# Block-diagonal compressed keys and values, a compression in two stretches, and a later place for the split of h, in a two-layer hybrid decoder trunk

## The chip, the cores and the metric

The kernel runs on one core of one Trainium2 chip. The metric is the device time of one execution, in microseconds. The engines by their names in the profile: PE is the matrix engine (PEld its weight loads), DVE the vector engine, ACT the scalar engine, POOL the GpSimd engine, and SP the engine that issues most DMAs. Each engine takes its instructions in the order in which the program has them.

## The reference, cut to what matters

256 positions of width 1024 go through two layers; each layer is a SwiGLU half-step, a token mixer and a second SwiGLU half-step. All is float32.

```python
def swiglu(x, w_gate, w_up, w_down):
    return (silu(x @ w_gate) * (x @ w_up)) @ w_down      # D_FF = 2816

for l in range(2):
    x = x + 0.5 * swiglu(rms_norm(x, norm_ffn1[l]), ...)
    x = x + hybrid_mixer(rms_norm(x, norm_mix[l]), ...)
    x = x + 0.5 * swiglu(rms_norm(x, norm_ffn2[l]), ...)
return rms_norm(x, norm_final)
```

The mixer has four groups of four heads of 64: forgetting attention (fox), native sparse attention (NSA), sliding-window (swa) and dilated attention (dil). NSA sums three gated branches; the one that the change touches is the compressed branch. Its keys and values are 15 compressed positions, made by a small MLP over windows of 32 positions, and all four heads share them:

```python
blocks = concat(chunks[:-1], chunks[1:]) + cmp_pe[idx]        # 15 windows of 32 positions x 64
kc, vc = silu(blocks . cmp_w1[idx]) @ cmp_w2[idx]             # 15 x 64, once for k, once for v
p_cmp = masked_softmax(q . kc / 8 - slope * dist, dist >= 0)  # 256 x 15 for each of 4 heads
o_cmp = gate0 * (p_cmp @ vc)
```

## The kernel before, in words

The positions are two halves (h = 0 and 1) of 128 rows. Every weight matrix is cut into sets of 256 rows by up to 512 columns. For each set, SP loads `wraw` (one of four buffers), ACT rounds it to a high part `whi` (fp32r), DVE computes the rest, `wlo` (line 115 is `split`, lines 119 to 121, which does both; line 149 is the matmul of `Set.mm`). The activations are split alike (`xhi`, `xlo`, `hhi`, `hlo`), and a product is the sum of three matmuls for each 128 rows: hi by hi, hi by lo and lo by hi. A set is so six matmuls for one half, twelve for both. Sets are split two ahead of their use (`AHEAD`), and the work of half 1 follows that of half 0 by five sets (`LAG`). A tile `whi` or `wlo` is free for a new set when half 1 has used the old one.

An FFN goes in 11 chunks of 256 hidden columns. A chunk is four sets of gate and up (`gate_up`, accumulating in the bank `ps_g`) and two sets of down for the chunk two before it (`down_`, banks `ps_d`). After the fourth gate-up set, ACT computes SiLU (line 318, `sg`), DVE multiplies (line 319), and the product h must be turned before it is an operand of down. In chunks 0, 1 and 10 PE turns it (`turn`, line 290). In the eight others it goes a far way (`turn_far`): DVE transposes blocks of 32 (`z`, line 298), POOL writes four pieces to DRAM (`far`, line 301) and reads them back (`pT`, line 305), and after a counted number of steps (`BACK`) the split of h is written into the program:

```python
            yield BACK
            back = back.rearrange("p (a k i) -> p k a i", a=4, k=2)
            hT[h, c] = tuple(hbuf.tile([P, 2, P], F32R, name=f"h{t}{h}") for t in ("hi", "lo"))
            split(back, *(t.rearrange("p k (a i) -> p k a i", a=4) for t in hT[h, c]))
```

A tile scheduler then places the instructions of each engine by a modelled due time; `tc.issue_after(x)` makes it place what stands under it behind x on the same engine.

The mixer projects its input by the sets of `win` and runs the attention beside them: generators (`attend`, `compress`, `cmp_branch`, ...) advance by one step with each set. `attend` computes scores (line 399, two heads at a time in 64-row halves of the array), a softmax, scaling by 1/sum (DVE), four transposes (line 445), a copy to `pT` (line 448) and the products with the values (line 457). `compress` loads four pieces of `cmp_w1` into `wraw` buffers, with eight matmul pairs for each (line 497), and makes from them `kc` and `vc` (lines 504 to 520). `idle` (line 95) is the operand of the matmuls that warm PE up at the start.

Of the kernel before, what the change touches and what calls it, by code (L numbers as in the profile page):

```python
# [15 lines left out]
P = 128  # L16
# [6 lines left out]
NB = 15  # L23
# [32 lines left out]
def hybrid_kernel(ctx: ExitStack, tc: tile.TileContext, a: dict, out: bass.AP):  # L56
# [27 lines left out]
    tbl = {g: const.tile([P, 4, 2 * P], F32, name=f"tbl_{g}") for g in ("nsa", "swa", "dil")}  # L84
    tbl["tri"] = const.tile([P, P], F32, name="tbl_tri")
# [9 lines left out]
    idle = const.tile([P, P], mybir.dt.bfloat16, name="idle")  # L95
    nc.vector.memset(idle, 0.0)
# [14 lines left out]
    def keep(engine, f, *args, **kw):  # L111

        last = fixed.get(engine)
        with tc.issue_after(last.ins) if last is not None else nullcontext():
            ins = f(*args, **kw)  # L115
        if engine in fixed:
            fixed[engine] = ins

    def split(pt, hi, lo):
        keep("ACT", nc.scalar.activation, hi, pt, AF.Copy)  # L120
        keep("DVE", nc.vector.tensor_tensor, lo, pt, hi.bitcast(F32), op=ALU.subtract)

    class Set:
# [5 lines left out]
        def load(self, parts=1):  # L129
# [8 lines left out]
            for k in ks:  # L138
                yield
                split(r[:, k], self.hi[:, k], self.lo[:, k])  # L140
# [140 lines left out]
    def add_ffn(norm, gu, down, nxt):  # L281
# [12 lines left out]
        def turn_far(h, c, hh):  # L294
# [14 lines left out]
            split(back, *(t.rearrange("p k (a i) -> p k a i", a=4) for t in hT[h, c]))  # L309
# [34 lines left out]
    def add_mixer(l, norm, nxt):  # L344
# [57 lines left out]
        def softmax(h, views, table, nk, sink=None, guard=False):  # L402

            p = work.tile([P, 4, P * (h + 1)], F32, name=f"p{h}")[:, :, :nk]
# [77 lines left out]
        def compress():  # L482
# [8 lines left out]
            for q in range(4):  # L491
                w1 = raw.tile([P, 2, 512], F32, name="wraw").rearrange("p j (c e) -> p j c e", e=P)
                nc.sync.dma_start(w1, a["w1"][l, q])
                yield 2
                for j in range(2):
                    for c in range(4):
                        nc.tensor.matmul(part[32 * c:32 * c + NB, :P], blk[:, c // 2, 8 * (c % 2) + 2 * q + j, :],
                                         w1[:, j, c, :], start=q == 0 and j == 0, stop=q == 3 and j == 1)
# [18 lines left out]
            kc = small.tile([P, NB], F32, name="kc", bufs=1)  # L517
            nc.vector.tensor_copy(kc, cp[:, :NB])
            M["vc"] = small.tile([NB, 64], F32, name="vc", bufs=1)
            nc.vector.tensor_copy(M["vc"], cp[:NB, 64:128])  # L520
            M["kc"] = kc

        def cmp_branch(h):
            while "kc" not in M:
                yield 1
# [334 lines left out]
```

## Time and profile before

| what | value |
|---|---|
| time, median of 3 runs | 1019.8 us (1019.18 to 1020.0) |
| time of the profiled execution | 1020.97 us |
| its span in the profile | 1019.2 us |
| PE busy | 996.3 us (98%) |
| DVE, ACT, POOL busy | 642.0, 515.8, 195.0 us |
| DMA | 200.36 MB, 197 GB/s on average |
| mean granted clock of PE | 0.995 |

The time of an execution is the span and 1.8 us around it. The profiled execution lies 1.2 us above the median of the three runs. A row of the timeline begins with its start and its duration in us; a matmul of 512 columns is shown for 0.39 us, but matmuls are pipelined, so what counts is the distance from one start to the next. In brackets stands how long the engine had been idle, and what ended that.

### The profile page before, as it was taken

The numbers are of one execution on the slowest core, as the hardware profiler recorded it, in microseconds if no ns is written. First come the engines' busy times: TensorE is split into PE (matmuls) and PEld (weight loads), VectorE is DVE, ScalarE is ACT, GpSimd is POOL, SyncE is SP. The second block draws the span as 40 slices with busy tenths as digits, with TensorE's granted clock in tenths as the row PEclk, the third lists the DMA queues.
The fourth block names the chain that finished last, engine by engine and source line by source line (L and its number), as shares of the span: only waits on it lengthen the run. The fifth ranks groups of instructions, "written<-read, shape, count | busy, mean of one in ns | idle before, by whom it ended". The sixth has DMA issues, their size and how long they took to land.

```text
span 1019.2 us, 14178 instructions
## 1 busy us (share of the span) xinstructions
PE 996.3 (98%) x4899; PEld 801.4 (79%) x4899; DVE 642.0 (63%) x1223; ACT 515.8 (51%) x886; POOL 195.0 (19%) x351
## 2 busy tenths in 40 slices
PE   8999999999999999999999999999999999999997
PEld 5788787867778888788878888878678788888875
DVE  6565656786777456465755565648776775656464
ACT  6444444554665445354644454446466564445452
POOL 0132323010000023332102232310100001323230
PEclk9999999999999999999999999999999999999999
DMA  8677767644354466676656777755634455677671
GB/s 294 235 224 262 235 220 244 207 151 166 119 166 139 154 212 215 219 221 237 204 175 202 222 229 224 235 186 176 189 109 155 128 166 190 205 234 214 220 232 47
DMA packets 68855, 200.36 MB, mean 197 GB/s; under 512 B 12448, under 2 KB 20528, under 8 KB 68784
## 3 DMA queue, kind: packets, MB, share of 16 engines
q1 hardware_dynamic: 56352, 180.83, 55.1%
q0 software_dynamic: 11712, 17.86, 5.4%
q8 instruction: 38, 0.62, 0.3%
q10 hardware_dynamic: 720, 0.79, 0.2%
q14 instruction: 33, 0.27, 0.1%
HBM read 189.98 MB, written 9.45 MB: 196 GB/s over the span
## 4 chain that ended last, share of the span: by engine, by line
PE 40%; DMA 26%; DVE 11%; POOL 9%; issue 7%; ACT 7%; POOLq 0%; SPq 0%; ACTq 0%; DVEq 0%
PE ps_g L149 22%; DMA far<-z 13%; DMA pT<-far 11%; PE ps_d L149 10%; POOL far L301 9%; DVE wlo L115 5%; ACT whi L115 4%; PE ps_t L457 2%; DVE sg L319 2%; DMA wraw<-in_gu 1%; PE ps_t L445 1%; DVE z L298 1%; PE ps_d L399 1%; PE ps_t L379 1%; PE ps_t L262 1%
## 5 line engine op out<-in xcount | busy, mean ns | idle before, releaser
L115 DVE TENSOR_TENSOR wlo<-wraw,whi 128x1024 fp32r<-128x1024 f32 (+3 forms) x329 | 392.4, 1196 | 176.6 <-ACT whi L115 175.6
L115 ACT ACTIVATE whi<-wraw 128x1024 fp32r<-128x1024 f32 (+3 forms) x329 | 341.0, 1038 | 224.9 <-PE ps_g L149 105.4
L149 PE MATMUL ps_g<-whi,xhi 128*128 128x512 f32 (+2 forms) x896 | 352.0, 394 | 5.8 <-ACT whi L115 3.8
L149 PE MATMUL ps_g<-wlo,xhi 128*128 128x512 f32 (+2 forms) x896 | 347.5, 388 | 3.7 <-DVE wlo L115 3.6
L149 PE MATMUL ps_g<-whi,xlo 128*128 128x512 f32 (+2 forms) x896 | 346.4, 387 | 0.0
L149 PEld LDWEIGHTS ps_g<-whi,xhi 128*128 128x128 f32 x896 | 168.6, 188 | 47.5 <-ACT whi L115 6.7
L301 POOL DMA_DIRECT2D far<-z x256 | 139.8, 554 | 327.4 <-DVE z L298 322.8
L149 PEld LDWEIGHTS ps_g<-wlo,xhi 128*128 128x128 f32 x896 | 168.7, 188 | 37.3 <-DVE wlo L115 6.8
L149 PEld LDWEIGHTS ps_g<-whi,xlo 128*128 128x128 f32 x896 | 168.5, 188 | 31.7 <-DVE xlo L115 0.5
L149 PE MATMUL ps_d<-whi,hhi 128*128 128x512 f32 x352 | 138.9, 395 | 0.0
L149 PE MATMUL ps_d<-whi,hlo 128*128 128x512 f32 x352 | 137.8, 391 | 0.0
L149 PE MATMUL ps_d<-wlo,hhi 128*128 128x512 f32 x352 | 137.6, 391 | 0.0
L115 ACT ACTIVATE hhi<-pT 128x256 fp32r<-128x256 f32 x64 | 26.7, 417 | 153.4 <-DMA pT<-far 153.4
L115 DVE TENSOR_TENSOR hlo<-pT,hhi 128x256 fp32r<-128x256 f32 x64 | 27.2, 425 | 107.5 <-ACT hhi L115 107.4
L149 PEld LDWEIGHTS ps_d<-whi,hlo 128*128 128x128 f32 x352 | 66.4, 189 | 13.9
L149 PEld LDWEIGHTS ps_d<-wlo,hhi 128*128 128x128 f32 x352 | 66.6, 189 | 13.6
L149 PEld LDWEIGHTS ps_d<-whi,hhi 128*128 128x128 f32 x352 | 66.5, 189 | 13.4
L159 POOL TENSOR_TENSOR rstd<-ms,mhalf 128x1 f32<-128x1 f32 x14 | 8.6, 614 | 291.4 <-DVE ms L157 291.4
L305 POOL DMA_DIRECT2D pT<-far x64 | 35.6, 557 | 142.4 <-DMA far<-z 111.9
L318 ACT ACTIVATE sg<-ps_g,rstd 128x256 f32<-128x256 f32 x88 | 41.1, 467 | 22.4 <-PE ps_g L149 22.1
L319 DVE SCALAR_TENSOR_TENSOR sg<-ps_g,rstd,sg 128x256 f32<-128x256 f32 x88 | 42.1, 478 | 15.8 <-ACT sg L318 15.8
L416 ACT ACTIVATE p<-p,nm 128x128 f32<-128x128 f32 (+2 forms) x96 | 40.1, 419 | 22.8 <-DVE nm L408 10.5
(158 smaller groups left out, 654.4 us busy)
## 6 DMA issues: line engine op xcount, KB each, us to landing
wraw<-in_gu SPq DMA_DIRECT2D x175, 512.0 KB, 4.1
wraw<-in_down SPq DMA_DIRECT2D x88, 512.0 KB, 4.5
wraw<-in_win SPq DMA_DIRECT2D x24, 512.0 KB, 4.0
far<-z POOLq DMA_DIRECT2D x256, 32.0 KB, 4.0
pT<-far POOLq DMA_DIRECT2D x64, 128.0 KB, 3.7
wraw<-in_wout SPq DMA_DIRECT2D x16, 512.0 KB, 3.5
wraw<-in_win SPq DMA_DIRECT2D x16, 384.0 KB, 3.6
wraw<-in_w SPq DMA_DIRECT2D x8, 512.0 KB, 3.5
```

What stands on the lines that cost most here:

```text
L115: ins = f(*args, **kw)
L149: nc.tensor.matmul(acc, x_[k], w[:, k, :], start=first and i == 0, stop=last and i == 5)
L262: nc.tensor.transpose(pt[:, j, :], xg[:, j * P:(j + 1) * P], ident)
L298: nc.vector.transpose(st, hh)
L301: nc.gpsimd.dma_start(far[:, :, a_, :].rearrange("b j e -> j b e"), st[32 * a_:32 * a_ + 32].rearrange("j (b e) -> j b e", b=4))
L305: nc.gpsimd.dma_start(back, far.rearrange("b j a e -> (b j) (a e)"))
L318: nc.scalar.activation(sg, acc[h][:, :256], AF.Silu, scale=r)
L319: nc.vector.scalar_tensor_tensor(sg, acc[h][:, 256:], r, sg, op0=ALU.mult, op1=ALU.mult)
L379: nc.tensor.transpose(pt[:, j, :], z[:, j * P:(j + 1) * P], ident)
L399: nc.tensor.matmul(dst, qT[r, i // 2, :], keys(i)[r, :nk], start=True, stop=True)
L416: nc.scalar.activation(p[:, i, :], p[:, i, :], AF.Exp, bias=nm[:, i:i + 1], scale=-1.0, accum_out=den[:, i:i + 1])
L457: nc.tensor.matmul(o[64 * e:64 * e + 64, j, :], vals(2 * j + e, n), pts[n][:w, 2 * j + e, :], start=n == 0, stop=n == len(blocks) - 1)
```

## The change

It has four parts.

1. In the far chunks the split of h is tied to the split of the set that was split last when the program comes to that point: `split` and `keep` now return their ACT instruction, each set keeps it as `last`, and `turn_far` issues h's split under `tc.issue_after`.
2. The compressed branch. `kc` becomes a tile of 128 x 2 x 15 in which the keys of the even heads stand in rows 0 to 63 and those of the odd heads in rows 64 to 127, in columns of their own, the rest zero. `vc` becomes a 128 x 256 tile with the values in four blocks, at rows 32 i and at the columns of head i, the rest zero. The probabilities of the four heads stand side by side in a constant tile `pc`, 32 columns for each head. So the scores take one matmul for two heads, the transposes become one of 128 x 128, and the products with the values one matmul for two heads. The scaling by 1/sum is one DVE instruction over four heads instead of four.
3. `compress` loads two pieces of `cmp_w1` and then runs the matmuls of both, and does so twice, where before each of the four pieces had its matmuls one step after its load.
4. The warm-up matmuls read the zeroed tile `ph` instead of a tile of their own.

```diff
--- before.py
+++ after.py
@@ -82,6 +82,8 @@
     ph = const.tile([P, P], F32, name="ph")
     nc.gpsimd.memset(ph, 0.0)
     tbl = {g: const.tile([P, 4, 2 * P], F32, name=f"tbl_{g}") for g in ("nsa", "swa", "dil")}
+    pc = const.tile([P, 4, 32], F32, name="pc")
+    nc.gpsimd.memset(pc, 0.0)
     tbl["tri"] = const.tile([P, P], F32, name="tbl_tri")
     tbl["cmp"] = const.tile([P, 2, 4, NB], F32, name="tbl_cmp")
 
@@ -92,8 +94,7 @@
                 nc.sync.dma_start(tbl[g] if dst is None else dst, a[f"c_{g}"])
 
 
-    idle = const.tile([P, P], mybir.dt.bfloat16, name="idle")
-    nc.vector.memset(idle, 0.0)
+    idle = ph.bitcast(mybir.dt.bfloat16)[:, :P]
     one = const.tile([P, 1], F32, name="one")
     nc.vector.memset(one, 1.0)
     heat = bank("t")
@@ -115,10 +116,12 @@
             ins = f(*args, **kw)
         if engine in fixed:
             fixed[engine] = ins
+        return ins
 
     def split(pt, hi, lo):
-        keep("ACT", nc.scalar.activation, hi, pt, AF.Copy)
+        first = keep("ACT", nc.scalar.activation, hi, pt, AF.Copy)
         keep("DVE", nc.vector.tensor_tensor, lo, pt, hi.bitcast(F32), op=ALU.subtract)
+        return first
 
     class Set:
 
@@ -137,7 +140,7 @@
                 self.dma = nc.sync.dma_start(r[:, k], self.src[:, k])
             for k in ks:
                 yield
-                split(r[:, k], self.hi[:, k], self.lo[:, k])
+                self.last = split(r[:, k], self.hi[:, k], self.lo[:, k])
 
         def mm(self, acc, hi, lo, first, last):
             xs = ((hi, self.hi), (hi, self.lo), (lo, self.hi))
@@ -306,7 +309,8 @@
             yield BACK
             back = back.rearrange("p (a k i) -> p k a i", a=4, k=2)
             hT[h, c] = tuple(hbuf.tile([P, 2, P], F32R, name=f"h{t}{h}") for t in ("hi", "lo"))
-            split(back, *(t.rearrange("p k (a i) -> p k a i", a=4) for t in hT[h, c]))
+            with tc.issue_after(sets[done[0] - 1].last.ins):
+                split(back, *(t.rearrange("p k (a i) -> p k a i", a=4) for t in hT[h, c]))
 
         def gate_up(h, c, s, st):
             if s == 0:
@@ -399,9 +403,10 @@
                 nc.tensor.matmul(dst, qT[r, i // 2, :], keys(i)[r, :nk], start=True, stop=True)
             return views
 
-        def softmax(h, views, table, nk, sink=None, guard=False):
-
-            p = work.tile([P, 4, P * (h + 1)], F32, name=f"p{h}")[:, :, :nk]
+        def softmax(h, views, table, nk, sink=None, guard=False, p=None):
+
+            if p is None:
+                p = work.tile([P, 4, P * (h + 1)], F32, name=f"p{h}")[:, :, :nk]
             nm = small.tile([P, 4], F32, name="nm")
             den = small.tile([P, 4], F32, name="den")
             for i in (0, 2, 1, 3):
@@ -488,14 +493,17 @@
                     nc.vector.tensor_tensor(blk[r, v], src,
                                             M["pe"][r, v, :].unsqueeze(2).to_broadcast([64, 16, NB]), op=ALU.add)
             part = bank("d1")
-            for q in range(4):
-                w1 = raw.tile([P, 2, 512], F32, name="wraw").rearrange("p j (c e) -> p j c e", e=P)
-                nc.sync.dma_start(w1, a["w1"][l, q])
-                yield 2
-                for j in range(2):
-                    for c in range(4):
-                        nc.tensor.matmul(part[32 * c:32 * c + NB, :P], blk[:, c // 2, 8 * (c % 2) + 2 * q + j, :],
-                                         w1[:, j, c, :], start=q == 0 and j == 0, stop=q == 3 and j == 1)
+            for qs in ((0, 1), (2, 3)):
+                w1 = []
+                for q in qs:
+                    w1.append(raw.tile([P, 2, 512], F32, name="wraw").rearrange("p j (c e) -> p j c e", e=P))
+                    nc.sync.dma_start(w1[-1], a["w1"][l, q])
+                    yield 2
+                for q in qs:
+                    for j in range(2):
+                        for c in range(4):
+                            nc.tensor.matmul(part[32 * c:32 * c + NB, :P], blk[:, c // 2, 8 * (c % 2) + 2 * q + j, :],
+                                             w1[q % 2][:, j, c, :], start=q == 0 and j == 0, stop=q == 3 and j == 1)
             for c in range(4):
                 r = slice(32 * c, 32 * c + NB)
                 nc.vector.tensor_copy(ph[r], part[r, :P])
@@ -514,17 +522,43 @@
             nc.tensor.matmul(cp[:, :NB], M["w2"][:, 0:2, :].rearrange("p t d -> p (t d)"), hid[:, 0, :],
                              start=True, stop=True)
             nc.tensor.matmul(cp[:NB, 64:128], hid[:, 1, :], M["w2"][:, 2, :], start=True, stop=True)
-            kc = small.tile([P, NB], F32, name="kc", bufs=1)
-            nc.vector.tensor_copy(kc, cp[:, :NB])
-            M["vc"] = small.tile([NB, 64], F32, name="vc", bufs=1)
-            nc.vector.tensor_copy(M["vc"], cp[:NB, 64:128])
+
+            kc = small.tile([P, 2, NB], F32, name="kc", bufs=1)
+            nc.gpsimd.memset(kc, 0.0)
+            M["vc"] = work.tile([P, 2, 16, NB], F32, name="blk", bufs=1).rearrange("p a b c -> p (a b c)")[:, :256]
+            nc.gpsimd.memset(M["vc"], 0.0)
+            for e in range(2):
+                r = slice(64 * e, 64 * e + 64)
+                nc.vector.tensor_copy(kc[r, e, :], cp[r, :NB])
+            for i in range(4):
+                c = 128 * (i // 2) + 64 * (i % 2)
+                nc.vector.tensor_copy(M["vc"][32 * i:32 * i + NB, c:c + 64], cp[:NB, 64:128])
             M["kc"] = kc
 
         def cmp_branch(h):
+
             while "kc" not in M:
                 yield 1
-            yield from attend(h, lambda: M["nq", h], lambda i: M["kc"], lambda i: tbl["cmp"][:, h, i, :],
-                              lambda i, n: M["vc"], put_part(h, False, True), NB, f"d{h}", gate=0, guard=True)
+            s = bank(f"d{h}")[:, :4 * NB].rearrange("p (j e k) -> p j e k", j=2, e=2)
+            for j in range(2):
+                nc.tensor.matmul(s[:, j].rearrange("p e k -> p (e k)"), M["nq", h][:, j, :],
+                                 M["kc"].rearrange("p e k -> p (e k)"), start=True, stop=True)
+            p, rd = softmax(h, [s[:, :, e, :] for e in range(2)], lambda i: tbl["cmp"][:, h, i, :], NB,
+                            guard=True, p=pc[:, :, :NB])
+            w = small.tile([P, 4], F32, name="gw")
+            nc.vector.tensor_tensor(w, rd, M["gate", h][:, 0::3], op=ALU.mult)
+            nc.vector.tensor_tensor(p, p, w.unsqueeze(2).to_broadcast([P, 4, NB]), op=ALU.mult)
+            yield 3 + 2 * h
+            yield 0
+            pt = bank("t")
+            nc.tensor.transpose(pt[:, :P], pc.rearrange("p i k -> p (i k)"), ident)
+            sb = work.tile([P, 4, P], F32, name="pT")[:, 0, :]
+            nc.scalar.activation(sb, pt[:, :P], AF.Copy)
+            yield 2
+            o = bank("t")[:, :256].rearrange("p (j t) -> p j t", j=2)
+            for j in range(2):
+                nc.tensor.matmul(o[:, j, :], M["vc"][:, P * j:P * j + P], sb, start=True, stop=True)
+            put_part(h, False, True)(o)
 
         def log_sigmoid(h, z, r):
```

ACT early in the first FFN, before. `hhi1` and `hhi0` are the high parts of an h of half 1 and of one of half 0, both from the far way (`pT`); `sg` are two SiLUs:

```order
L115 ACTIVATE whi_608<-wraw_607 128x1024
L115 ACTIVATE hhi1_694<-pT_577 128x256
L115 ACTIVATE whi_627<-wraw_626 128x1024
L115 ACTIVATE hhi0_704<-pT_586 128x256
L115 ACTIVATE whi_645<-wraw_644 128x1024
L318 ACTIVATE sg_662<-ps_g_600,rstd_227 128x256
L115 ACTIVATE whi_673<-wraw_672 128x1024
L318 ACTIVATE sg_684<-ps_g_613,rstd_199 128x256
L115 ACTIVATE whi_709<-wraw_708 128x1024
```

The same nine rows after the change:

```order
L116 ACTIVATE whi_608<-wraw_607 128x1024
L116 ACTIVATE whi_627<-wraw_626 128x1024
L116 ACTIVATE whi_645<-wraw_644 128x1024
L322 ACTIVATE sg_662<-ps_g_600,rstd_227 128x256
L116 ACTIVATE whi_673<-wraw_672 128x1024
L116 ACTIVATE hhi1_694<-pT_577 128x256
L322 ACTIVATE sg_684<-ps_g_613,rstd_199 128x256
L116 ACTIVATE hhi0_704<-pT_586 128x256
L116 ACTIVATE whi_709<-wraw_708 128x1024
```

`hhi1` passed three `whi` and a `sg`, `hhi0` two `whi` and both `sg`.

DVE at the same place, before (`hlo` is the low part of h, `z` the blockwise transpose of the product that begins the far way):

```order
L115 TENSOR_TENSOR hlo1_695<-pT_577,hhi1_694 128x256
L115 TENSOR_TENSOR wlo_628<-wraw_626,whi_627 128x1024
L115 TENSOR_TENSOR hlo0_705<-pT_586,hhi0_704 128x256
L115 TENSOR_TENSOR wlo_646<-wraw_644,whi_645 128x1024
L319 SCALAR_TENSOR_TENSOR sg_662<-ps_g_600,rstd_227,sg_662 128x256
L298 STREAM_TRANSPOSE z_665<-sg_662 128x256
L115 TENSOR_TENSOR wlo_674<-wraw_672,whi_673 128x1024
L319 SCALAR_TENSOR_TENSOR sg_684<-ps_g_613,rstd_199,sg_684 128x256
L298 STREAM_TRANSPOSE z_687<-sg_684 128x256
L115 TENSOR_TENSOR wlo_710<-wraw_708,whi_709 128x1024
```

And after:

```order
L116 TENSOR_TENSOR wlo_646<-wraw_644,whi_645 128x1024
L323 SCALAR_TENSOR_TENSOR sg_662<-ps_g_600,rstd_227,sg_662 128x256
L301 STREAM_TRANSPOSE z_665<-sg_662 128x256
L116 TENSOR_TENSOR wlo_674<-wraw_672,whi_673 128x1024
L323 SCALAR_TENSOR_TENSOR sg_684<-ps_g_613,rstd_199,sg_684 128x256
L116 TENSOR_TENSOR hlo1_695<-pT_577,hhi1_694 128x256
L301 STREAM_TRANSPOSE z_687<-sg_684 128x256
L116 TENSOR_TENSOR hlo0_705<-pT_586,hhi0_704 128x256
L116 TENSOR_TENSOR wlo_710<-wraw_708,whi_709 128x1024
```

`hlo1` now stands between the second product and its `z`, and `hlo0` behind that `z`.

PE where half 0 has its compressed scores in the first layer, before (`ps_d0<-kc`), and where their transposes and those of another head group stand:

```order
L149 MATMUL ps_g_2334<-whi_2027,xhi11_1796 128x512
L149 MATMUL ps_g_2334<-wlo_2028,xhi11_1796 128x512
L399 MATMUL ps_d0_2374<-kc_2370,qT_1928 128x15
L399 MATMUL ps_d0_2375<-kc_2370,qT_1928 128x15
L399 MATMUL ps_d0_2374<-kc_2370,qT_1928 128x15
L399 MATMUL ps_d0_2375<-kc_2370,qT_1928 128x15
L149 MATMUL ps_g_2334<-whi_2027,xlo11_1797 128x512
L379 MATMUL ps_t_2422<-ident_86,z_2413 128x128 x2
L399 MATMUL ps_d1_2444<-kT_win_1808,qT_2110 128x256
L379 MATMUL ps_t_2422<-ident_86,z_2413 128x128 x2
L445 MATMUL ps_t_2430<-ident_86,p1_2315 128x128 x4
```

After:

```order
L152 MATMUL ps_g_2334<-whi_2027,xhi11_1796 128x512
L152 MATMUL ps_g_2334<-wlo_2028,xhi11_1796 128x512
L152 MATMUL ps_g_2334<-whi_2027,xlo11_1797 128x512
L544 MATMUL ps_d0_2380<-kc_2370,qT_1928 128x30 x2
L383 MATMUL ps_t_2421<-ident_86,z_2412 128x128 x2
L403 MATMUL ps_d1_2443<-kT_win_1808,qT_2110 128x256
L403 MATMUL ps_d1_2444<-kT_win_1808,qT_2110 128x256
L450 MATMUL ps_t_2429<-ident_86,p1_2315 128x128 x4
```

The four score matmuls have become two, one matmul of the projection later, and stand next to the transposes of line 379 (383 after).

PE at the second piece of `cmp_w1`, before (`ps_d1<-wraw,blk`; line 445 are transposes of the window branch):

```order
L445 MATMUL ps_t_2194<-ident_86,p0_2133 128x128
L149 MATMUL ps_g_2032<-whi_2084,xhi01_1727 128x512
L564 MATMUL ps_t_2095<-upper_89,lf_2078 4x128
L445 MATMUL ps_t_2194<-ident_86,p0_2133 128x128 x3
L149 MATMUL ps_g_2032<-wlo_2085,xhi01_1727 128x512
L149 MATMUL ps_g_2032<-whi_2084,xlo01_1728 128x512
L149 MATMUL ps_g_2032<-whi_2084,xhi01_1727 128x512
L149 MATMUL ps_g_2032<-wlo_2085,xhi01_1727 128x512
L149 MATMUL ps_g_2032<-whi_2084,xlo01_1728 128x512
L497 MATMUL ps_d1_2117<-wraw_2179,blk_2112 15x128 x8
L149 MATMUL ps_g_2152<-whi_1901,xhi11_1796 128x512
L149 MATMUL ps_g_2152<-wlo_1902,xhi11_1796 128x512
```

After:

```order
L152 MATMUL ps_g_2032<-whi_2084,xhi01_1727 128x512
L152 MATMUL ps_g_2032<-wlo_2085,xhi01_1727 128x512
L450 MATMUL ps_t_2186<-ident_86,p0_2133 128x128
L152 MATMUL ps_g_2032<-whi_2084,xlo01_1728 128x512
L598 MATMUL ps_t_2095<-upper_89,lf_2078 4x128
L450 MATMUL ps_t_2186<-ident_86,p0_2133 128x128 x3
L152 MATMUL ps_g_2032<-whi_2084,xhi01_1727 128x512
L152 MATMUL ps_g_2032<-wlo_2085,xhi01_1727 128x512
L152 MATMUL ps_g_2032<-whi_2084,xlo01_1728 128x512
L505 MATMUL ps_d1_2117<-wraw_2118,blk_2112 15x128 x8
L505 MATMUL ps_d1_2117<-wraw_2171,blk_2112 15x128 x8
L152 MATMUL ps_g_2152<-whi_1901,xhi11_1796 128x512
```

The first group of eight matmuls, which stood some rows earlier, is now together with the second.

## Rows read from the trace of the kernel before

**Rows 1.** Page, part 1: busy time, share of the span, instructions of PE.

```profile
PE 996.3 (98%) x4899; PEld 801.4 (79%) x4899; DVE 642.0 (63%) x1223; ACT 515.8 (51%) x886; POOL 195.0 (19%) x351
```

**Rows 2.** Waits: engine, line, releaser; us in total, times, longest.

```profile
ACT hhi L115 <- DMA pT<-far: 153.4, 59, 6.6
...
PE ps_g L149 <- ACT whi L115: 3.8, 4, 2.0
PE ps_g L149 <- DVE wlo L115: 3.6, 6, 0.8
```

**Rows 3.** Timeline of PE, second FFN, a place with two waits.

```profile
415.94 0.39 PE L149 MATMUL ps_g<-whi,xlo 128*128 128x512 f32 x1
417.06 0.49 PE L149 MATMUL ps_g<-whi,xhi 128*128 128x512 f32 x1 [0.74 <-ACT whi L115]
418.32 0.50 PE L149 MATMUL ps_g<-wlo,xhi 128*128 128x512 f32 x1 [0.76 <-DVE wlo L115]
418.66 0.39 PE L149 MATMUL ps_g<-whi,xlo 128*128 128x512 f32 x1
```

**Rows 4.** Timeline of ACT, the same place.

```profile
415.65 0.42 ACT L115 ACTIVATE hhi<-pT 128x256 fp32r<-128x256 f32 x1 [6.38 <-DMA pT<-far]
415.97 1.04 ACT L115 ACTIVATE whi<-wraw 128x1024 fp32r<-128x1024 f32 x1
```

**Rows 5.** Timeline of PE, the first and last of the FFN waits.

```profile
102.52 0.50 PE L149 MATMUL ps_g<-wlo,xhi 128*128 128x512 f32 x1 [0.17 <-DVE wlo L115]
...
969.17 0.50 PE L149 MATMUL ps_g<-wlo,xhi 128*128 128x512 f32 x1 [0.76 <-DVE wlo L115]
```

**Rows 6.** Windows: us, busy time (x) of each engine, granted PE clock, DMA share, GB/s.

```profile
671.50:675.00 3.50, 3.50 (x11) 2.72 (x10) 2.81 (x5) 0.98 (x3) 1.87 (x4) 0.52 0.82 282
```

**Rows 7.** Timeline of ACT and PE, an FFN chunk without a wait of PE.

```profile
65.93 0.42 ACT L115 ACTIVATE hhi<-pT 128x256 fp32r<-128x256 f32 x1 [3.45 <-DMA pT<-far]
...
72.30 1.06 ACT L115 ACTIVATE whi<-wraw 128x1024 fp32r<-128x1024 f32 x1 [0.92 <-ACT sg L318]
...
87.01 0.39 PE L149 MATMUL ps_d<-whi,hhi 128*128 128x512 f32 x1
```

**Rows 8.** Timeline of DVE and PE, end of the first FFN.

```profile
189.97 0.68 DVE L278 SCALAR_TENSOR_TENSOR x<-ps_d,x 128x512 f32<-128x512 f32 x1
...
191.91 0.47 PE L149 MATMUL ps_d<-whi,hhi 128*128 128x512 f32 x1
```

**Rows 9.** Timeline of PE, first mixer: compressed scores, transposes and products of half 0.

```profile
248.07 0.40 PE L149 MATMUL ps_g<-wlo,xhi 128*128 128x512 f32 x1
248.39 0.62 PE L399 MATMUL ps_d<-kc,qT 64*128 64x15 f32 x8
248.94 0.50 PE L149 MATMUL ps_g<-whi,xlo 128*128 128x512 f32 x1
...
254.42 0.61 PE L445 MATMUL ps_t<-ident,p 128*15 128x128 f32 x4
254.79 0.47 PE L149 MATMUL ps_g<-whi,xhi 128*128 128x512 f32 x1
...
258.84 0.65 PE L457 MATMUL ps_t<-pT,vc 15*64 15x128 f32 x8
259.42 0.50 PE L149 MATMUL ps_g<-whi,xhi 128*128 128x512 f32 x1
```

**Rows 10.** Timeline of PE, first mixer: the matmul with `pick`, a full array.

```profile
243.34 0.38 PE L504 MATMUL ps_d<-pick,ph 128*128 128x30 f32 x2 [0.26 <-DVE nm L408]
243.56 0.47 PE L149 MATMUL ps_g<-whi,xlo 128*128 128x512 f32 x1
```

**Rows 11.** Timeline of PE, first mixer: compression and the wait before it.

```profile
227.54 0.30 PE L445 MATMUL ps_t<-ident,p 128*128 128x128 f32 x1 [0.85 <-DVE lsp L548]
...
229.96 0.63 PE L497 MATMUL ps_d<-wraw,blk 128*15 128x128 f32 x16
```

**Rows 12.** Timeline of DVE, first mixer: copy of the compressed keys.

```profile
247.60 0.17 DVE L518 COPY kc<-ps_d 128x15 f32<-128x15 f32 x1
```

## The prediction

> **What bounds the kernel now.** The busy times come first: PE is busy for 98% of the span, no other engine above 63% [rows 1]. So only PE's idle time, its slow time and its own work can be saved, and what another engine does counts where PE waits for it. The view of waits comes second. It names two groups in the FFN and the projections, for whi (3.8 us, of which 2.0 us is one wait at the start of the program, before any h exists) and for wlo (3.6 us in 6) [rows 2]. ACT itself waits 153.4 us for the DMA that brings h back (`hhi <- DMA pT<-far`), 59 times, up to 6.6 us [rows 2]. That is harmless while nothing urgent stands behind the hhi. The timelines come third, and there the reader sees that it isn't always harmless. In the second FFN ACT is idle for 6.38 us until the far DMA has landed, starts hhi at 415.65, and only then whi at 415.97, which ends at 417.01 [rows 4]; PE, idle since the matmul of 415.94, starts at 417.06 [rows 3]. Then hhi0 takes ACT once more ahead of the next whi (the order of ACT shows it), and PE waits 0.76 us for wlo. All nine FFN waits have this form: three for whi, 1.8 us without the one at the start, and six for wlo; the first of them is at 102.52 and the last at 969.17 [rows 5].
>
> **The FFN part of the change.** It moves hhi1 behind three whi and a sg, and hhi0 behind two whi and both sg. The whi that was stuck behind a DMA is then released by PE alone.
> What the waits cost: the idle time of the nine is 1.8 + 3.6 = 5.4 us. The cost is more, since a restarted matmul stream begins slowly. In rows 3 the starts go from 415.94 to 418.66, 2.72 us for three matmuls that take 3 x 0.227 = 0.68 us at the usual distance, so 2.04 us are lost for 1.50 us of idle. By that ratio 5.4 us are 7.3 us. The waits alone in their place carry more surplus, about 0.15 us for the entry and 0.11 us behind it (0.34 us from 418.32 to 418.66 instead of 0.227) [rows 3]; with the surplus taken wait by wait I get 8.0 us, and use that. Bounds: 5.4 (idle alone) and 8.0.
> A second term hangs on one of these places. After a wait of the same form at 668 to 671 the granted clock is 0.52 of full speed for 3.5 us, that is the 1.2 GHz level for nearly all of it [rows 6], and PE was busy all of it, so 3.5 x 0.48 = 1.7 us are lost. Without the wait that slow time goes too. Bounds 0 and 1.7.
> The Trainium skill ("TensorE: Matmul & The Clock Gate", section "What's actually happening") has a reason: idle time of the engine brings the 1.2 GHz level back, at a moment that isn't tied to the kernel's start. By that rule this term differs from execution to execution; the trace shows it behind one of two like places only (clock normal behind 418.66).
>
> What is late next. hhi and hlo are used a chunk later: the hhi at 65.93 is first an operand at 87.01 [rows 7], and the new place is about 5 us later (ACT is done with the sg ahead of it at 72.30 - 0.92 = 71.4), so 16 us remain. ACT is idle for 0.92 us ahead of its whi at 72.30 [rows 7], and two hhi at 0.33 us from start to start (415.65 to 415.97 [rows 4]) fit into that. On DVE hlo1 and hlo0 now stand around the second z, each about as long as the 0.42 us of a hhi [rows 4], whose size they have. The whi of 72.30 ends at 73.4, its wlo behind hlo0 near 75.1 by my estimate, and PE needs that at 77.5 by its sequence of 12 x 0.227 = 2.72 us per set. The DMA: in the worst place shown it landed at 415.65, and the new place there is some 2.2 us later, counted from the set that PE was then at. So no wait is left in the new place on the landings of this trace. The second z starts 0.42 us later than now, and its far DMA with it; this comes out of the 2.2 us.
> At the end of each FFN there is less room. The last far split is tied behind the x split there: hlo1 falls behind the residual that starts on DVE at 189.97 and takes 0.68 us, so it ends near 191.1, and the down matmul that takes hlo is the second after that of 191.91 [rows 8], at 192.4. Still no wait, but the next norm's product on DVE comes 0.42 us later, and the transposes of it may cost PE 0.1 us in each of four FFNs: 0.4 us lost, bounds 0 and 0.6.
>
> **The compressed branch**, four times (two layers, two halves). Scores: the row of eight takes 248.94 - 248.39 = 0.55 us, the entry 0.32 - 0.23 = 0.09 more [rows 9], and the matmul behind a row like this 0.11 more (as in rows 3): 0.75 us. Eight records are four fp32 matmuls. After the change they are two, so four records, on a full array. The nearest row is the matmul with `pick`, two records in 0.22 us [rows 10], so four in 0.43 us and 0.1 behind: 0.22 us saved. Transposes: four in 0.37 us [rows 9], one in 0.09: 0.28 us saved. Products with the values: eight records in 0.58 us [rows 9]. Four full-array records with 128 columns have no row; by rows 10 they take 0.43 us, and if each takes as long as two of the present ones, 0.58 us. I take 0.48, 0.10 us saved, bounds 0 (even -0.1 if the larger weight tile isn't covered) and 0.15. Sum 0.60 us per call, 2.4 us in all; bounds 1.4 and 3.0.
> That the halved count is worth so little has a cause that the rows show: eight records with 64 rows take 0.07 us each, two with 128 rows 0.11 us each [rows 9, 10].
> The Trainium skill ("TensorEngine Tiling (Array Packing)", sections "Theoretical Speedup" and "Key Properties") speaks here on both sides. Independent tiles of 64 rows run side by side and give up to 2x, so the zeros of the blocks cost what the tiles gave: by that alone four matmuls become two at no gain, and the branch would save only the 1.1 us of the transposes. The same page says that a change of tiling mode drains the engine, which the change then spares; the 0.09 us of entry in rows 9 agrees, and by that the scores gain as I count them.
>
> **The compression.** Two pieces now share one entry and one restart. That is 0.2 us for the second pair, in two layers: 0.4 us, bounds 0 and 0.5. The first pair gains nothing: its matmuls of the first piece leave a stretch in which PE waits anyway for DVE (0.85 us at 227.54 [rows 11], the row of the second piece is at 229.96), and DVE's order there is the same, so PE gets to the wait earlier and waits longer. The raw buffers are held longer, so the third piece and a win set are loaded later on SP; the whi of that set moves by about 2 us to near 234, and PE needs it near 240.
> Copies of kc and vc on DVE become six instead of two; at the 0.17 us of the present one [rows 12] this is 0.5 to 0.7 us for each layer, ahead of the z that PE will transpose. DVE's saving of three scalings stands against it. PE has projection matmuls before it; I count 0, bounds -0.6 (a wait in each layer) and 0. The memsets on POOL and the warm-up's operand lie beside work of others; 0.
>
> **Sum.** 8.0 + 1.7 - 0.4 + 2.4 + 0.4 = 12.1 us off the profiled execution's own 1020.97 us, 1008.9 us. The runs shown have a median of 1019.8, 1.2 us less than that one. If that is the execution as such, the forecast is 1007.7; if those runs just lack the slow clock, it is 1019.8 - 10.4 = 1009.4. I say 1008.5. With all low bounds (5.4 + 0 - 0.6 + 1.4 - 0.6 = 5.6) the time is 1014.2, with all high bounds (8.0 + 1.7 + 3.0 + 0.5 = 13.2) 1006.6; for the likeliest case 1006 to 1011.
>
> **Rivals.**
> A, the waits come back in part. ACT now meets hhi1 just ahead of a sg; if the smoother loading shifts the far DMAs by 2 to 3 us against the sets, some of the nine waits return at 1.0 us each, or new ones at the end of the FFN. For it: the room is 2.2 us at the worst place and ACT's longest wait for such a landing is 6.6 us [rows 2]. Against it: most of the 59 waits ended long before the new place. Four to six waits kept, and the slow clock: 1011 to 1017.
> B, no change. The nine waits were slack that PE pays elsewhere: it would have to wait for DMA or DVE behind them. Against it: DVE is 63% busy, and PE waits for no raw load in the list. 1018 to 1021.8.
> C, slower. The far way feeds on itself: hlo1 stands ahead of the second z on DVE, so a late landing delays that z, its far DMA and the next chunk's landing. From the point where the landing is later than its new place by more than the 2.4 us that DVE has (75.1 against 77.5), the chunk's sg, z and wlo are late for PE, and then the next chunk's as well. Price: 32 far chunks by at least the 0.42 us of hlo is 13.4 us, less the 2.8 us of the mixer and compression, on 1019.8: 1030, and with half of the chunks 1024. For it only the order on DVE; against it the room of 2.2 us in the worst place.
> D, a larger gain: the mixer's waits go as well, 1004 to 1006.
>
> **Chances.** Forecast 0.65, A 0.17, B 0.09, C 0.07, D 0.02. A measurement of this kernel tells about 0.2% or 2 us from no change. Faster: 0.65 + 0.17 + 0.02 = 0.84; same 0.09; slower 0.07. The range 1005 to 1016.5 leaves out B, C and the ends of A and D.
>
> **What will show it.** Right: in the waits, PE for whi and wlo falls from 7.4 to about 2 us (the start), ACT's wait for `pT<-far` falls far below 153 us, and no low clock behind an FFN wait. In the compressed branch rows of four records in about 0.43 and 0.48 us, and one transpose. Wrong, if PE has new waits for sg, hlo or xn, if ACT's hhi still waits for DMA with whi behind it, or if the value products take more than 0.6 us.

## The result and the profile after

The changed kernel takes 1006.44 us (median of 3 runs, 1006.43 to 1006.48) against 1019.8 us: a ratio of 0.987, 95% interval 0.985 to 0.989, 13.4 us less. Forecast were 1008.5 us and 1005 to 1016.5. The profiled execution took 1006.48 us, with a span of 1004.4 us; it is 14.5 us shorter than the profiled one of before. The gain in the medians, 13.4 us, lies just past the sum of all high bounds of the prediction (13.2).

PE's waits after the change (us in total, times, longest; all rows of 0.6 us or more but for the warm-up's):

```profile
PE ps_g L152 <- ACT whi L116: 3.3, 2, 2.9
PE ps_t L450 <- DVE lsp L582: 2.0, 2, 1.1
PE ps_t L450 <- DVE p L442: 1.0, 2, 0.5
...
PE ps_t L560 <- ACT pT L453: 0.9, 2, 0.5
PE ps_g L152 <- DVE ge L640: 0.7, 2, 0.5
PE ps_d L403 <- DVE kT_slc L658: 0.6, 2, 0.4
```

The two waits for whi are at the start of the program (5.58 and 8.97); no wait for wlo is left, and among ACT's waits the 153.4 us for h's DMA [rows 2] are gone. The row of an FFN is now this, in the order of ACT (beside [rows 4]):

```profile
412.86 1.05 ACT L116 ACTIVATE whi<-wraw 128x1024 fp32r<-128x1024 f32 x1
413.81 0.40 ACT L116 ACTIVATE hhi<-pT 128x256 fp32r<-128x256 f32 x1
414.12 0.46 ACT L322 ACTIVATE sg<-ps_g,rstd 128x256 f32<-128x256 f32 x1
414.47 0.41 ACT L116 ACTIVATE hhi<-pT 128x256 fp32r<-128x256 f32 x1
```

No hhi has a bracket: its data is there. What that is worth is best read in windows. Each runs from the last turn of chunk 1 on PE to the first of chunk 10, the same 561 or 562 matmul groups in all four FFNs (us, PE busy, granted clock, DMA share, GB/s). Before:

```profile
44.60:174.06 129.46, 127.92 (x562) 1.00 0.71 234
358.80:487.59 128.79, 127.29 (x561) 1.00 0.69 222
545.55:676.14 130.59, 128.90 (x561) 0.99 0.70 221
861.34:989.88 128.54, 127.53 (x562) 1.00 0.70 221
```

After:

```profile
44.72:171.45 126.73, 126.73 (x562) 1.00 0.75 242
354.92:481.65 126.73, 126.73 (x561) 1.00 0.72 226
538.14:664.88 126.74, 126.74 (x562) 1.00 0.73 227
848.56:975.29 126.73, 126.73 (x562) 1.00 0.73 226
```

PE is now busy all of the time there, and the four stretches agree within 0.01 us. The compressed branch (beside [rows 9]) has the rows that were forecast; here those of half 0 in the first layer:

```profile
245.68 0.40 PE L152 MATMUL ps_g<-whi,xlo 128*128 128x512 f32 x1
245.91 0.53 PE L544 MATMUL ps_d<-kc,qT 128*128 128x30 f32 x4
246.28 0.41 PE L383 MATMUL ps_t<-ident,z 128*128 128x128 f32 x2
...
252.10 0.39 PE L152 MATMUL ps_g<-wlo,xhi 128*128 128x512 f32 x1
252.44 0.30 PE L554 MATMUL ps_t<-ident,pc 128*128 128x128 f32 x1
252.50 0.47 PE L152 MATMUL ps_g<-whi,xlo 128*128 128x512 f32 x1
...
255.99 0.61 PE L560 MATMUL ps_t<-pT,blk 128*128 128x128 f32 x4
256.36 0.48 PE L152 MATMUL ps_g<-whi,xhi 128*128 128x512 f32 x1
```

From start to start: 0.37 us for the scores, 0.06 for the transpose, 0.37 for the products with the values. The transpose stands by itself now, so the matmul ahead of it takes 0.34 instead of 0.23.

A ledger over the profiled executions, cut at the turns of h on PE (starts of the rows of lines 290 and 293):

| part | before | after | saved |
|---|---|---|---|
| start, to chunk 1 of the first FFN | 44.60 | 44.72 | -0.12 |
| four FFN stretches as above | 517.38 | 506.93 | 10.45 |
| two mixers, from an FFN's last turn to chunk 0 of the next | 292.85 | 290.10 | 2.75 |
| what lies between (ends and beginnings of FFNs) | 148.96 | 147.39 | 1.57 |
| after the last turn | 15.4 | 15.3 | 0.1 |

### The profile page after: what moved, and what is told of

The parts are those of the page before. It is cut to its first block, busy times and chain, and to the rows that moved or that the text cites. A ratio compares the mean times of both kernels' runs of the same rounds, so it can differ in the third digit from the quotient of the medians.

```text
span 1004.4 us, 14094 instructions
## 1 busy us (share of the span) xinstructions
PE 987.4 (98%) x4855; PEld 801.0 (80%) x4855; DVE 641.0 (64%) x1218; ACT 515.3 (51%) x886; POOL 196.6 (20%) x356
## 4 chain that ended last, share of the span: by engine, by line
PE 88%; DVE 5%; ACT 3%; DMA 2%; issue 1%; SPq 0%; POOLq 0%; ACTq 0%; DVEq 0%
PE ps_g L152 53%; PE ps_d L152 27%; DVE wlo L116 2%; DMA wraw<-in_win 2%; PE ps_t L462 1%; PE ps_t L450 1%; ACT whi L116 1%; PE ps_d L403 1%; PE ps_t L265 1%; ACT p L421 1%; DMA wraw<-in_gu 1%; PE ps_t L383 1%; ACT sq L156 1%; PE ps_t L403 1%; PE ps_t L293 1%
## 5 line engine op out<-in xcount | busy, mean ns | idle before, releaser
L152 PEld LDWEIGHTS ps_d<-wlo,hhi 128*128 128x128 f32 x352 | 66.1, 188 | 13.4
L421 ACT ACTIVATE p<-p,nm 128x128 f32<-128x128 f32 (+1 forms) x80 | 35.5, 445 | 19.8 <-DVE nm L417 10.3
L301 DVE STREAM_TRANSPOSE z<-sg 128x256 f32<-128x256 f32 x64 | 28.4, 443 | 1.3
L156 ACT ACTIVATE sq<-x 128x512 bf16<-128x512 f32 (+1 forms) x29 | 17.6, 608 | 17.8 <-DVE x L281 17.7
```

The source lines that it names most:

```text
L152: nc.tensor.matmul(acc, x_[k], w[:, k, :], start=first and i == 0, stop=last and i == 5)
L156: nc.scalar.activation(sq[:, :sl.stop - sl.start], x[h][:, sl], AF.Square, scale=1.0 / 32.0, accum_out=stat)
L301: nc.vector.transpose(st, hh)
L421: nc.scalar.activation(p[:, i, :], p[:, i, :], AF.Exp, bias=nm[:, i:i + 1], scale=-1.0, accum_out=den[:, i:i + 1])
```

## The experiments

The runs came in three groups, each on a chip of its own, and the kernel before had a median of 1019.08, 1016.0 and 1018.7 us on them. Times are compared within a group.

**The parts alone.** The tie alone is

```diff
+            with tc.issue_after(sets[done[0] - 1].last.ins):
                 split(back, *(t.rearrange("p k (a i) -> p k a i", a=4) for t in hT[h, c]))
```

with `last` and the returned instructions; `no_tie` is the changed kernel without these two lines; `block_only` and `stretch_only` take over parts 2 and 4, and part 3, of the change.

> The kernel before with the tie of h's split alone. Theory (ACT's queue): whi stood behind a hhi that waited for its DMA; with the tie all of these waits go, the one that showed as a wait for xn at 501.72 too, and the late order of xlo ahead of xn at 516.83: 10 to 11 us off 1019.8, so 1009.3 (1008.5 to 1010.3); PE's waits for whi and wlo only at the start. Rival (the mixer carries more than I counted): 1012 or more.

> The changed kernel without the tie, that is with the block-diagonal branch, the two stretches and the shared warm-up operand. Theory: the FFN waits are back, 1019.8 - 2.8 = 1017.0 (1016.3 to 1018). Rival (the mixer carries more): 1012 to 1015. The parts should add up: what this saves and what the tie alone saves make 13.4 us together.

> The kernel before with the block-diagonal branch and the shared warm-up operand alone. Theory: 0.60 us for each of four calls, 2.4 us off: 1017.4. Rival (small tiles run side by side, so halving the matmuls gains nothing, only the transposes do): 1.1 us off, 1018.7.

> The kernel before with the compression in two stretches alone. Theory: one entry and one restart saved in each layer, 0.4 us: 1019.4. Rival (the later loads on SP or the longer wait for DVE take it back): 1019.8 or more.

| kernel | median, us | lowest to highest | ratio to before, interval |
|---|---|---|---|
| before | 1019.08 | 1015.41 to 1024.77 | |
| tie_only | 1009.26 | 1008.64 to 1010.01 | 0.990 (0.987 to 0.992) |
| no_tie | 1015.87 | 1010.96 to 1019.15 | 0.996 (0.994 to 0.998) |
| block_only | 1014.35 | 1012.65 to 1016.36 | 0.995 (0.993 to 0.997) |
| stretch_only | 1019.87 | 1016.06 to 1022.85 | 1.000 (0.998 to 1.001) |

The tie alone is worth 9.8 us, and what is left without it 3.2; together 13.0. `tie_only` lies in the range of its theory. `no_tie` lies 0.4 us under the lower end of its own, which was counted from 1019.8 us, and the kernel before took 0.7 us less on this chip. `block_only` gained 4.7 us, about twice what its theory said, and `stretch_only` came out at its rival's time. The table shows something else: every kernel without the tie scatters by 3.7 to 9.4 us (9 to 26 runs of each), the one with it by 1.4 (5 runs). In its trace the first FFN stretch is

```profile
43.17:169.93 126.76, 126.76 (x562) 1.00 0.76 242
```

and its other three take 126.7 us each, while the stretches of the four kernels without the tie take 127.3 to 131.0 us. ACT's wait for h's DMA in `no_tie`, and what PE pays for it:

```profile
PE ps_g L152 <- DVE wlo L116: 5.5, 9, 0.8
...
ACT hhi L116 <- DMA pT<-far: 153.8, 57, 6.6
```

So how many of the landings are late differs from one FFN to the next in one trace. That it also differs from execution to execution would explain the scatter; there is one trace of each kernel, so this is not shown directly. In any case 1 us between two executions of the kernel before says nothing. For the branch and the stretches apart, that scatter is too large: 4.7 us for the branch alone but 3.2 for both can't be read as a cost of the stretches.

**The stretches and the scores, with the tie in place.** `no_stretch` takes part 3 back. `scores_old` takes the two full-array score matmuls back, and keeps the rest:

```diff
-            s = bank(f"d{h}")[:, :4 * NB].rearrange("p (j e k) -> p j e k", j=2, e=2)
-            for j in range(2):
-                nc.tensor.matmul(s[:, j].rearrange("p e k -> p (e k)"), M["nq", h][:, j, :],
...
+            s = scores(M["nq", h], lambda i: M["kc"][:, i % 2, :], NB, f"d{h}")
```

> The changed kernel with the four pieces of the compression one by one again (tie and block-diagonal branch kept), so that the stretches can be read without the scatter of the FFN waits. By the sum of the prediction the two stretches are worth 0.4 us: 1006.8. By the four runs so far (the branch alone 4.7 us, branch and stretches together 3.2) they cost 1 us or more: 1005.5 or less.

> The changed kernel with the compressed scores as before, four matmuls on 64-row halves of the array and two banks, but with the block-diagonal values and the one transpose. By my sum the two full-array score matmuls save 0.22 us in each of four calls: 1007.3. By the rule that two small tiles run side by side they save nothing: 1006.4, or 1006.1 with the larger weight tile as a cost.

On one chip `no_stretch` took 1004.8 us (1004.13 to 1005.78), `scores_old` 1007.56 (1006.6 to 1009.8); the changed kernel wasn't run on that chip, and the kernel before is 3.8 us faster there than the 1019.8 us from which the expectations were counted, so `no_stretch` is taken up again below. The two mixers of the changed kernel take 290.10 us, those of `scores_old` 292.12, 2.0 us more. With the distances around them, the four rows of scores alone make about 1.2 us of that (0.55 against 0.37 us for a row, the rest in its entry and the matmul behind). Another 0.4 us is PE's wait for kT_slc (1.0 against 0.6 us). So the full-array scores save more than the 0.9 us of the sum, and here the tiles side by side did cost more than the full array.

**Place or program?** Two kernels move the split by the counted steps alone, with `BACK = 10` changed to 13 in the kernel before, and to 8 in the changed one.

> The kernel before with the split of h three steps later in the program (BACK 13 instead of 10), without the tie. ACT's order still has hhi one row behind the third whi, since the scheduler moves it up. Theory (the place in ACT's order decides): no change, 1019 (1017.5 to 1020.5), ACT still waits some 150 us for h's DMA. Rival (the program's position decides, or the moved reads of h land otherwise): 1012 or less.

> The changed kernel with BACK 8: h's split stays tied, but hhi stands right behind the third whi that it is tied to, directly ahead of the first sg, about 3 us earlier than in the changed kernel. Theory: the latest landings come about 1 us behind this place, ahead of sg but with no whi behind that PE needs at once: 1006.4 to 1008. Rival C of the prediction (a late hlo delays z, far and the next chunk): over 1010.

`before_back13`: 1017.22 us (1013.85 to 1018.8), before 1016.0 on that chip, ratio 1.001 (1.000 to 1.002). No change, as the place in ACT's order hadn't changed; ACT still waits for h's DMA, and PE behind it:

```profile
PE ps_g L149 <- DVE wlo L115: 4.3, 7, 0.8
...
ACT hhi L115 <- DMA pT<-far: 137.4, 52, 6.4
```

So it's the order on ACT that counts and not where the split is written. `after_back8`: 1007.22 us (1006.57 to 1009.46). Its hhi stand about 3 us earlier in the cycle, and ACT meets a late landing again, eight times:

```profile
ACT hhi L116 <- DMA pT<-far: 4.7, 8, 2.0
```

None of it reaches PE (its FFN stretches sum to 507.13 us, against 506.93); behind these hhi stands a sg and not a whi that PE needs next.

**One row earlier still.** 

> The changed kernel with BACK 6: hhi is tied one whi behind its place in the kernel before and ahead of the fourth whi again. Theory: the whi behind it is blocked by late landings as before, though by about one set's 2.7 us less, so some waits of about 1 us come back: 1007.5 to 1012, and scatter with them. Rival (the tie as such, not the place, removed the waits): as the changed kernel, within 0.5 us.

`after_back6` took 1022.26 us (1017.04 to 1029.58), before 1018.7, ratio 1.003 (1.000 to 1.006): worse than I expected, and slower than the kernel before, by an amount that is small beside its scatter. Its profile is of the longest of its executions, the one of 1029.58 us. Waits there:

```profile
PE ps_d L152 <- DVE wlo L116: 8.3, 11, 0.8
PE ps_t L293 <- DVE sg L323: 3.2, 4, 1.0
PE ps_d L152 <- ACT whi L116: 3.0, 6, 1.3
...
ACT hhi L116 <- DMA pT<-far: 107.4, 51, 4.4
```

ACT waits less than before (107 us against 153) and PE more: 14.5 us in these three rows, where the nine FFN waits of the kernel before make 5.4. A place in the second FFN, rows of DVE, ACT and PE:

```profile
422.26 0.45 DVE L301 STREAM_TRANSPOSE z<-sg 128x256 f32<-128x256 f32 x1
```

```profile
435.08 0.42 ACT L116 ACTIVATE hhi<-pT 128x256 fp32r<-128x256 f32 x1 [3.52 <-DMA pT<-far]
435.40 1.04 ACT L116 ACTIVATE whi<-wraw 128x1024 fp32r<-128x1024 f32 x1
```

```profile
436.50 0.50 PE L152 MATMUL ps_d<-whi,hhi 128*128 128x512 f32 x1 [0.21 <-ACT whi L116]
437.76 0.51 PE L152 MATMUL ps_d<-wlo,hhi 128*128 128x512 f32 x1 [0.76 <-DVE wlo L116]
```

```profile
440.12 0.45 DVE L301 STREAM_TRANSPOSE z<-sg 128x256 f32<-128x256 f32 x1
```

From the second z of a chunk (422.26) to the landing (435.08) are 12.8 us, and from there to the next chunk's second z (440.12) 5.0 us more, through the whi behind it, two sg and their products: 17.9 us, while a chunk takes 16.32 us in the changed kernel (its z at 70.67 and 86.99, for one). So a late landing delays the whi, the sg, the z and so the next landing: four chunks in a row, up to the z of 475.85, take 17.8 to 18.5 us. This is the loop of rival C of the prediction, at another place than the changed kernel's and through ACT's order instead of hlo on DVE. There the two hhi of a chunk, first that of half 1, then that of half 0, stand 14.3 and 15.0 us behind that z (70.97 and 71.62, behind 56.65). Seven traces have landings on which ACT waited, 343 in all. Counted in the same way, those of half 1 came 7.7 to 12.3 us behind the z and those of half 0 9.1 to 14.0 us. So the room is about 2 us for half 1, as I had read from one landing of half 1 in one trace, but only 1.0 us for half 0.

**One chip for the changed kernel and two that beat it.** `pair_second` joins only the third and the fourth piece:

```diff
-            for qs in ((0, 1), (2, 3)):
+            for qs in ((0,), (1,), (2, 3)):
...
-                                             w1[q % 2][:, j, c, :], start=q == 0 and j == 0, stop=q == 3 and j == 1)
+                                             w1[q - qs[0]][:, j, c, :], start=q == 0 and j == 0, stop=q == 3 and j == 1)
```

> The changed kernel unaltered, beside the next three on one chip, since the kernel before differs between chips by 3 us. It should come out 9 to 13 us under the kernel before, with less scatter than that, at 1005 to 1006.5.

> The changed kernel with the four pieces of the compression one by one. The prediction's term says 0.4 us slower than the changed kernel; the lengths of the two mixers in the traces so far (289.30 us here, 290.10 in the changed kernel) say 0.8 us faster. Within 0.2 us: the stretches are worth nothing.

> The changed kernel with only the third and the fourth piece of the compression in one stretch, the first two one by one. If the loss of the two stretches sits at the wait for lsp ahead of the first pair (0.96 and 1.07 us instead of 0.65 and 0.63) and the second pair saves its entry and restart, this is the fastest: 0.2 to 0.4 us under the one with four separate pieces. If the later loads on SP are the loss (PE waits for kT_slc), it is like the changed kernel.

| kernel | median, us | lowest to highest | two mixers in the trace |
|---|---|---|---|
| before | 1018.7 | 1015.2 to 1025.37 | |
| after_again | 1006.03 | 1005.21 to 1006.66 | 290.25 |
| no_stretch_2 | 1005.12 | 1004.63 to 1005.55 | 288.78 |
| pair_second | 1004.68 | 1003.53 to 1005.49 | 288.98 |

Both beat the changed kernel, and `pair_second` by 1.35 us; between the two the ranges overlap, and the traces don't part them. Aligned by the count of matmuls, `after_again` and `no_stretch_2` are level again behind the first pair in the second layer (0.2 us apart, and 0.3 at the start of that mixer), so that pair is worth nothing, as forecast. They part in the stretch behind it. There the changed kernel (`after_again`) has, in the second layer:

```profile
739.38 0.70 PE L403 MATMUL ps_d<-kT_win,qT 64*128 64x256 f32 x4
740.04 0.66 PE L450 MATMUL ps_t<-ident,p 128*128 128x128 f32 x4
740.62 0.70 PE L403 MATMUL ps_d<-kT_win,qT 64*128 64x256 f32 x2
741.25 0.44 PE L383 MATMUL ps_t<-ident,z 128*128 128x128 f32 x2
741.62 0.70 PE L403 MATMUL ps_d<-kT_win,qT 64*128 64x256 f32 x2
742.24 0.66 PE L450 MATMUL ps_t<-ident,p 128*128 128x128 f32 x4
```

and `no_stretch_2`:

```profile
739.14 0.70 PE L403 MATMUL ps_d<-kT_win,qT 64*128 64x256 f32 x4
739.80 0.66 PE L450 MATMUL ps_t<-ident,p 128*128 128x128 f32 x4
740.29 0.38 PE L383 MATMUL ps_t<-ident,z 128*128 128x128 f32 x2
740.60 0.70 PE L403 MATMUL ps_d<-kT_win,qT 64*128 64x256 f32 x4
```

Two records of these scores, that is one matmul on one half of the array, take as long as four on both halves (0.63 and 0.63 us); so the last four, torn apart by two transposes, cost 0.6 us more. The first layer has the same two orders. `pair_second`, which joins the second pair and gains, has these scores in two groups of four. The torn rows (1.2 us in two layers) less the 0.4 us of the forecast leave 0.8 us, near the 0.9 us measured. In the first layer of `after_again` PE also waits 0.82 us for kT_slc, which it doesn't in `no_stretch_2`; the changed kernel's own trace has 0.37 us there.

## Why the prediction was right, point by point

**The FFN waits (8.0 us): right.** The stretches give 10.45 us, of which 1.7 are the slow clock, so 8.7 us for the waits. The experiments show the mechanism as told: the place on ACT decides, not the program's, and in the changed kernel's place no landing reaches PE. The tie as such isn't enough: `after_back6` has it, at an earlier place, and PE waits.

**The slow clock (1.7 us): right in size, an accident.** Of five more traces with such waits one has it (`after_back6`: clock 0.83 over the 10 us from 680, where its longest waits are, 1.35 and 0.76 us); behind waits of 1.17 and 0.76 us at 668 in `stretch_only` it is missing. That agrees with what the Trainium skill says ("TensorE: Matmul & The Clock Gate", section "What's actually happening"), that the moment isn't tied to the kernel's start. The 1.2 us between the profiled execution of before and its median, which I weighed at length, is inside the scatter of that kernel.

**The end of an FFN (-0.4 us): the step that failed.** It was put as a loss and was a gain of 1.57 us. The 0.1 us that each of the four FFNs was to lose doesn't show: apart from two places, the pieces that the ledger sums up as lying between agree with those of before within 0.07 us. In these two places something was overlooked, worth 0.4 and 1.0 us. At the end of the second FFN there was a tenth wait of the same cause, under another name: ACT in the kernel before,

```profile
496.57 0.42 ACT L115 ACTIVATE hhi<-pT 128x256 fp32r<-128x256 f32 x1 [3.37 <-DMA pT<-far]
```

held two whi back, these their wlo on DVE, these the residual, and PE waited at 501.72 for xn (0.32 us). And the tie changed an order on DVE at the beginning of the next FFN. Before, xlo (which waits for ACT) stands ahead of xn:

```profile
515.40 0.69 DVE L115 TENSOR_TENSOR xlo<-ps_t,xhi 128x512 fp32r<-128x512 f32 x1 [1.09 <-ACT xhi L115]
516.00 0.68 DVE L228 TENSOR_TENSOR xn<-x,gain 128x512 f32<-128x512 f32 x1
```

and PE waited 0.73 us at 516.83 for xn (the profile names ms, which ran between):

```profile
516.83 0.63 PE L262 MATMUL ps_t<-ident,xn 128*128 128x128 f32 x4 [0.73 <-DVE ms L157]
```

After, xn comes first:

```profile
508.01 0.69 DVE L231 TENSOR_TENSOR xn<-x,gain 128x512 f32<-128x512 f32 x1
...
509.78 0.69 DVE L116 TENSOR_TENSOR xlo<-ps_t,xhi 128x512 fp32r<-128x512 f32 x1 [1.08 <-ACT xhi L116]
```

and PE doesn't wait. `tie_only` has the new order too and `no_tie` the old one, so here the tie brought it. But a tie is neither needed nor enough for it: `before_back13` has the new order without a tie, and `after_back6` the old one with it. The order of the changed kernel shows this without any run.

**The compressed branch (2.4 us): right in kind, too small.** By the distances between starts in the two traces, with the rows ahead and behind, a call of half 0 saves 0.36 us at the scores, 0.09 at the transposes and 0.32 at the values, one of half 1 0.28, 0.33 and 0.13: 1.5 us for a layer, 3.0 us in all, the upper bound. The transposes of half 0 miss the forecast 0.28 us: they stood right behind other scores and needed no entry of their own, and the one transpose that replaces them stands between projection matmuls. The two mixers take 288.8 to 290.1 us in the three traces with the branch and without the stretches, and 292.9 to 294.2 in the three with neither, so about 4 us. Of what the rows leave open, 0.8 us is an order again. The kernel before tears the same eight kT_win records as above into two and six, in each layer:

```profile
249.59 0.70 PE L399 MATMUL ps_d<-kT_win,qT 64*128 64x256 f32 x2
251.02 1.13 PE L399 MATMUL ps_d<-kT_win,qT 64*128 64x256 f32 x6
```

They take 0.63 and 1.06 us to the next row, and the two groups of four in `no_stretch_2` 0.66 and 0.63. The row that I took as nearest gives 0.11 us for each record of the `pick` matmul; four records in a row take 0.09 each, and why is open. The rule of the Trainium skill that speaks against the change ("TensorEngine Tiling (Array Packing)", "Theoretical Speedup") doesn't hold here, as the row of scores itself fell from 0.55 to 0.37 us. Its neighbour, the drain at a change of mode ("Key Properties"), agrees with the 0.1 us of entry that went with the small tiles, and is the smaller part.

**The compression (0.4 us): wrong in sign.** Beside `no_stretch_2` it costs 0.9 us (1006.03 to 1005.12). The first pair was read rightly; what was missed is that the rows behind it come in another order, with kT_win in four, two and two. The lines of PE's order in the section on the change stop at the first four of these records; the torn ones come right behind them. The branch gave more than forecast and the compression 1.3 us less, and the two cancel in the mixers' sum, 2.75 us against 2.8: that agreement is luck.

**The rivals.** A and B are excluded by the flat FFN stretches. C's loop is real where the hhi of half 1 stands 5.6 us earlier in the cycle (8.7 us behind the z in `after_back6`, where it meets no late landing). D had the larger gain right in direction but not in its reason: the mixer's waits didn't go (PE waits for lsp 1.6 us before and 2.0 after), and what came on top came at the ends and beginnings of FFNs.

Open: why one landing of half 0 comes 9.1 us behind that z and another 14.0. No run changed the DMAs.

## What to carry to other kernels

An in-order engine that has both urgent work and work that waits for a round trip through DRAM should meet the second kind where it has landed in every trace, with non-urgent work behind it; compare the latest landing (here 12.3 us for one half and 14.0 for the other) with the place in the cycle (14.3 and 15.0 of 16.32 us). Waiting less is no aim: the kernel whose ACT waited 107 us was slower than the one with 153. When a change reaches a scheduler, read the order of all engines over the whole program, not around the edit: two of the three wrong terms here stood in it.

## What the runs showed of the hardware beyond that

Two half-array fp32 score records take as long as four on both halves (0.63 us), so here a row of such scores that another instruction splits in two costs double. The scatter of a kernel's time seems to come from its own program: the kernel before spread over 9.4 us on one chip (26 runs) and over 10.2 on another (17 runs), and with the split in the changed kernel's place 1.4 us there (5 runs) and 1.45 (6 runs); `scores_old`, which has that place too, spread over 3.2 (6 runs).
